# An embedding gather with position add: whole-sequence stores in place of half-sequence stores

## The chip, the cores and the metric

The kernel runs on one core of a Trainium2 chip. The metric is device time in microseconds (us) of a run. Five runs of the kernel before gave 177.66, 179.09, 178.35, 179.17 and 179.04 us: a median of 179.04.

## What is computed

32 sequences of 512 token indices pick rows of 512 floats (2 KB) from a table of 50,000 rows; the row of the token's position is added:

```
token_embed = embedding_table[indices]        # (32, 512, 512) f32
return (token_embed + position_embed)         # position_embed (512, 512)
```

There is no matrix product. 32 x 512 x 2 KB = 33.55 MB are read from the table and as many are written; all else is small.

## The kernel before, in words

**Tiling.** A sequence b is a tile ("slot") of 128 partitions by K = 4 rows by 512 floats: partition p holds tokens 4p to 4p+3, so that the 8 KB of a partition are contiguous in the output, and the 1 MB of a sequence too. There are 23 slots (SLOTS); sequence b uses slot b % 23, so only sequences 23 to 31 use a slot again, and those of 0 to 8.

**Order.** The unit of work is a pair (b, k): the 128 tokens of row k in every partition, 256 KB. The list `order` (lines 64 to 66) fixes the sequence of the 128 units, numbered g: first k = 0, 1 of sequences 0 to 3 (FIRST = 4), then k = 2, 3 of these, then k = 0 to 3 of each of the sequences 4 to 31. Everything is written out by hand; no scheduler moves it.

**POOL** (lines 118 to 138) issues one indirect DMA for each unit: it gathers 128 rows of 2 KB into the slot. Ten semaphores ("lanes") take turns, and gather g waits until gather g-10 has landed (line 138). Gather 0 waits for the first indices, gather 16 for the turned indices (line 123), and the first gather of sequence 23, g = 92, until all stores of sequences 0 to 8 have landed (line 126).

**DVE** (lines 141 to 155) copies the position rows once from SBUF to PSUM, turns the indices of all sequences with one transpose, and adds the position rows to each unit in place as soon as its gather has landed. Each add increments `s_add`.

**ACT** (lines 158 to 165) issues the stores, all on its own queue, from the list `stores` (lines 67 to 72): each entry says after how many adds, which sequence, at which row k, and how many rows. The queue is worked through in order, and each store waits for its count of `s_add` (line 165). In the kernel before a store is half a sequence: two rows k of each partition, 4 KB from each partition, 512 KB in all. The first halves of sequences 0 and 1, and all of sequence 31, are stored by single rows (256 KB). That makes 60 stores of 512 KB and 8 of 256 KB.

**Loads.** SP's queue loads the first sequence's indices, ACT's queue the position rows (two loads of 512 KB) and the other indices. At the end POOL clears semaphores after the last add, and ACT waits for the last stores (lines 169 to 175).

Of the kernel before, what the change touches and what calls it, by code (L numbers as in the profile page):

```python
# [1 line left out]

# [4 lines left out]

P = 128
K = 4
SLOTS = 23  # L10
LANES = 10
FIRST = 4
Q = 32


@with_exitstack
def kernel(
    ctx: ExitStack,
    tc: tile.TileContext,
    indices: bass.AP,  # L20
    embedding_table: bass.AP,
    position_embed: bass.AP,
    out: bass.AP,
):

    nc = tc.nc
    f32 = mybir.dt.float32
    i32 = mybir.dt.int32
    add = mybir.AluOpType.add

    B, S = indices.shape
    V, D = embedding_table.shape
    assert S == P * K and B == 32
    J = P // Q  # L40
    assert B == Q, "indices are turned in squares of 32"


    idx_words = indices.bitcast(i32)
    idx_first = idx_words[0:FIRST].rearrange("b (p w) -> p b w", p=P)
    idx_rows = idx_words.rearrange("b (j w) -> b j w", j=J)
    out_rows = out.rearrange("b (p k) d -> b p k d", k=K)
    pos_rows = position_embed.rearrange("(p k) d -> p k d", k=K)
    table = embedding_table[:, :]

    def sbuf(name, shape, dtype):
        return nc.alloc_sbuf_tensor(name, shape, dtype).ap()

    idx0 = sbuf("idx0", [P, FIRST, 2 * K], i32)
    idx_raw = sbuf("idx_raw", [P, 2 * Q * K], i32)
    idx_t = sbuf("idx_t", [P, K, B], i32)
    pos_sb = sbuf("pos_sb", [P, K, D], f32)
    slots = [sbuf(f"slot{n}", [P, K, D], f32) for n in range(SLOTS)]
    pos_ps = nc.alloc_psum_tensor("pos_ps", [P, K, D], f32).ap()

    half = K // 2
    order = [(b, k) for h in range(2) for b in range(FIRST)
             for k in range(h * half, (h + 1) * half)]
    order += [(b, k) for b in range(FIRST, B) for k in range(K)]
    stores = []
    for g, (b, k) in enumerate(order):
        if (b <= 1 and k < half) or b == B - 1:
            stores.append((g + 1, b, k, 1))  # L70
        elif k % half == half - 1:
            stores.append((g + 1, b, k + 1 - half, half))

    sems = []

    def sem(name):
        sems.append(nc.alloc_semaphore(name))
        return sems[-1]

    s_first, s_next, s_raw = sem("s_first"), sem("s_next"), sem("s_raw")  # L80
    s_pos = [sem(f"s_pos{h}") for h in range(2)]
    s_gather = [sem(f"s_gather{n}") for n in range(LANES)]

    reused = range(B - SLOTS)
    s_out, s_idx, s_ps = sem("s_out"), sem("s_idx"), sem("s_ps")
    s_add, s_rest, s_pool = sem("s_add"), sem("s_rest"), sem("s_pool")
    nums = [x.num for x in sems]
    assert nums == list(range(nums[0], nums[0] + len(nums)))
    early, late = range(nums[0], nums[-3]), range(nums[-3], nums[-1] + 1)

    def rounds(g):
        return 16 * (g // LANES + 1)

    def load(out, in_, done, engine=nc.scalar):
        return engine.dma_start(out=out, in_=in_).then_inc(done, 16)

    def load_pos(h):
        part = slice(h * half, (h + 1) * half)
        return load(pos_sb[:, part, :], pos_rows[:, part, :], s_pos[h])

    for ins in (
        load(idx0[:, 0, :], idx_first[:, 0, :], s_first, engine=nc.sync),
        load_pos(0),
    ):
        tc.no_tile_sem_insts.add(ins.ins.name)
    tc.close()
    tc.compile()


    load(idx0[:, 1:, :], idx_first[:, 1:, :], s_next)
    for j in range(J):
        load(idx_raw[j * B : (j + 1) * B, :], idx_rows[:, j, :], s_raw)
    load_pos(1)


    nc.gpsimd.wait_ge(s_first, 16)
    for g, (b, k) in enumerate(order):
        if g == half:  # L120
            nc.gpsimd.wait_ge(s_next, 16)
        if g == FIRST * K:
            nc.gpsimd.wait_ge(s_idx, 1)  # L123
        if b == SLOTS and k == 0:
            done = sum(1 for x in stores if x[1] in reused)
            nc.gpsimd.wait_ge(s_out, 16 * done)
        if b < FIRST:
            where = idx0[:, b, 2 * k : 2 * k + 1]
        else:
            where = idx_t[:, k, b : b + 1]  # L130
        ins = nc.gpsimd.indirect_dma_start(  # L131
            out=slots[b % SLOTS][:, k, :],
            out_offset=None,
            in_=table,
            in_offset=bass.IndirectOffsetOnAxis(ap=where, axis=0),
        ).then_inc(s_gather[g % LANES], 16)
        if g >= LANES:
            ins._wait_ge(s_gather[g % LANES], rounds(g - LANES))


    for g, (b, k) in enumerate(order):
        if g == 7:
            nc.vector.transpose(  # L143
                out=idx_t[:],
                in_=idx_raw[:].rearrange("r (q k w) -> r k q w", k=K, w=2)[:, :, :, 0],
            )._wait_ge(s_raw, 16 * J).then_inc(s_idx, 1)
        if b == 0:
            nc.vector.tensor_copy(out=pos_ps[:, k, :], in_=pos_sb[:, k, :])._wait_ge(  # L148
                s_pos[k // half], 16
            ).then_inc(s_ps, 1)  # L150
            nc.vector.wait_ge(s_ps, k + 1)
        part = slots[b % SLOTS][:, k, :]
        nc.vector.tensor_tensor(  # L153
            out=part, in0=part, in1=pos_ps[:, k, :], op=add
        )._wait_ge(s_gather[g % LANES], rounds(g)).then_inc(s_add, 1)


    rest = 0
    for adds, b, at, n in stores:
        done = s_out if b in reused else s_rest  # L160
        rest += b not in reused
        nc.scalar.dma_start(
            out=out_rows[b][:, at : at + n, :],
            in_=slots[b % SLOTS][:, at : at + n, :],
        )._wait_ge(s_add, adds).then_inc(done, 16)

    nc.gpsimd.wait_ge(s_add, len(order))
    nc.gpsimd.drain()  # L170
    nc.gpsimd.dma_reset(early)
    nc.gpsimd.sem_clear(early).then_inc(s_pool, 1)
    nc.scalar.wait_ge(s_pool, 1)
    nc.scalar.wait_ge(s_rest, 16 * rest)
    nc.scalar.sem_clear(late)

# [1 line left out]
_INS = ['indices', 'embedding_table', 'position_embed']  # L178
_OUTS = [((32, 512, 512), 'float32')]


# [23 lines left out]
```

## Time and profile before

| | |
|---|---|
| median of five runs | 179.04 us (177.66 to 179.17) |
| the profiled execution, its time | 179.19 us |
| its span in the profile | 173.9 us |
| POOL busy | 121.4 us, 70% of the span, 132 instructions |
| DVE busy | 90.6 us, 52%, 133 instructions |
| DMA | 68.34 MB in 21,059 packets, mean 393 GB/s |
| chain that ended last | POOL 68%, issue 23%, DMA 6%, DVE 1% |
| stores | 60 of 512 KB and 8 of 256 KB, on ACT's queue |

The span is what the profiler records of the program; the time of the execution is 5.3 us longer. The chain that ended last is followed back from the last instruction; "issue" in it is time in which an engine waited for nothing that the profile shows. In the rows by line, "xN" is the count, then come busy time and mean ns of one, then idle time before them and what ended it. In the rows by slice, each digit is a fortieth of the span, in tenths of busy time. The DMA engines are 16, shared by all queues; queue 0 is that of POOL's gathers, queue 10 that of ACT's DMAs, queue 1 SP's. In the stretches, a DMA share of over 1 comes from packets of one engine that overlap a little in the records.

### The profile page before, as it was taken

To read this page: it belongs to the slowest core of one execution; us is meant where nothing else is said; L and a number is where in the kernel's file an instruction comes from. 1 tells how busy PE (TensorE), PEld (TensorE's weight loads), DVE (VectorE), ACT (ScalarE), POOL (GpSimd) and SP (SyncE) were. 2 spreads that over 40 slices of the span, in tenths; PEclk is the share of its full clock that TensorE was granted. 3 is DMA by queue.
4 is the path that set the end of the run, shared out by engine and by line. 5 is a ranking of instruction groups with operands and counts; after the bars stand their busy time and mean duration, and the time that the engine had idled before them with its cause. 6 is when DMAs were issued, how large, how long until landed. Compare 5 with 4: busy or idle time off the path is not lost.

```text
span 173.9 us, 387 instructions
## 1 busy us (share of the span) xinstructions
DVE 90.6 (52%) x133; POOL 121.4 (70%) x132
## 2 busy tenths in 40 slices
DVE  0343945544645555564556555555555465546451
POOL 2777777777777777777777777777777777777400
DMA  4889999999999999999999999999999999999997
GB/s 137 277 268 366 302 360 408 400 397 417 418 414 411 421 418 418 418 417 420 420 419 418 417 419 420 415 418 418 413 419 415 419 418 419 414 417 419 417 420 272
DMA packets 21059, 68.34 MB, mean 393 GB/s; under 512 B 3776, under 2 KB 3904, under 8 KB 21056
## 3 DMA queue, kind: packets, MB, share of 16 engines
q0 software_dynamic: 10240, 33.56, 49.8%
q10 hardware_dynamic: 10672, 34.75, 49.4%
q1 hardware_dynamic: 144, 0.00, 0.0%
q14 instruction: 3, 0.02, 0.0%
HBM read 34.75 MB, written 33.55 MB: 393 GB/s over the span
## 4 chain that ended last, share of the span: by engine, by line
POOL 68%; issue 23%; DMA 6%; DVE 1%; POOLq 0%
POOL slot L131 68%; DMA slot<-in_embedding_table_dram,idx_t 5%; DMA idx<-in_indices_dram 1%; DVE slot L153 1%; POOLq L123 0%
## 5 line engine op out<-in xcount | busy, mean ns | idle before, releaser
L131 POOL DMA_INDIRECT slot<-in_embedding_table_dram,idx_t x112 | 105.9, 946 | 34.1 <-issue 34.1
L153 DVE TENSOR_TENSOR slot<-slot,pos_ps 128x512 f32<-128x512 f32 x128 | 87.8, 688 | 76.1 <-issue 55.3
L131 POOL DMA_INDIRECT slot<-in_embedding_table_dram,idx x16 | 15.3, 954 | 7.4 <-issue 4.6
L148 DVE COPY pos_ps<-pos_sb 128x512 f32<-128x512 f32 x4 | 2.8, 690 | 4.2 <-DMA pos_sb<-in_position_embed_dram 4.2
L143 DVE STREAM_TRANSPOSE idx_t<-idx_raw 128x128 int32<-128x128 int32 x1 | 0.4, 400 | 0.0
L189 POOL MEMSET const-float32-0.0<- 128x1 f32 x1 | 0.1, 98 | 0.2 <-issue 0.2
L189 POOL MEMSET const-uint8-127<- 128x1 uint8 x1 | 0.1, 118 | 0.0
L189 POOL MEMSET const-bfloat16-1.0<- 128x1 bf16 x1 | 0.1, 113 | 0.0
L189 POOL MEMSET const-float32-1.0<- 128x1 f32 x1 | 0.1, 104 | 0.0
## 6 DMA issues: line engine op xcount, KB each, us to landing
out_dram<-slot ACTq DMA_DIRECT2D x60, 512.0 KB
out_dram<-slot ACTq DMA_DIRECT2D x8, 256.0 KB
slot<-in_embedding_table_dram,idx_t POOLq DMA_INDIRECT x112
pos_sb<-in_position_embed_dram ACTq DMA_DIRECT2D x2, 512.0 KB, 3.4
slot<-in_embedding_table_dram,idx POOLq DMA_INDIRECT x16
idx_raw<-in_indices_dram ACTq DMA_DIRECT2D x4, 32.0 KB
idx<-in_indices_dram SPq DMA_DIRECT2D x1, 4.0 KB, 2.3
idx<-in_indices_dram ACTq DMA_DIRECT2D x1, 12.0 KB
```

What stands on the lines that cost most here:

```text
L131: ins = nc.gpsimd.indirect_dma_start(out=slots[b % SLOTS][:, k, :], out_offset=None, in_=table, in_offset=bass.IndirectOffsetOnAxis(ap=whe ...
L143: nc.vector.transpose(out=idx_t[:], in_=idx_raw[:].rearrange("r (q k w) -> r k q w", k=K, w=2)[:, :, :, 0],)._wait_ge(s_raw, 16 * J).then_ ...
L148: nc.vector.tensor_copy(out=pos_ps[:, k, :], in_=pos_sb[:, k, :])._wait_ge(s_pos[k // half], 16).then_inc(s_ps, 1)
L153: nc.vector.tensor_tensor(out=part, in0=part, in1=pos_ps[:, k, :], op=add)._wait_ge(s_gather[g % LANES], rounds(g)).then_inc(s_add, 1)
L189: nc = _bacc.Bacc("TRN2", target_bir_lowering=False, num_devices=1)
```

## The change

Sequences 5 to 27 are stored whole: one DMA of 1 MB after the fourth add, in place of two of 512 KB after the second and the fourth. A limit on the length of the last dimension (half x D x 4 = 4096) is given to all stores, so that the 8 KB of a partition go as two descriptors of 4 KB; the halves and single rows are not longer than that. Sequences 0 to 4 and 28 to 31 keep their stores, and gathers, adds, lanes and slots stay as they were. The number of stores that gather 92 waits for is counted from the list, so it follows.

```diff
     for g, (b, k) in enumerate(order):
         if (b <= 1 and k < half) or b == B - 1:
             stores.append((g + 1, b, k, 1))
+        elif FIRST < b < B - 4:
+            if k == K - 1:
+                stores.append((g + 1, b, 0, K))
         elif k % half == half - 1:
             stores.append((g + 1, b, k + 1 - half, half))
...
         nc.scalar.dma_start(
             out=out_rows[b][:, at : at + n, :],
             in_=slots[b % SLOTS][:, at : at + n, :],
+            max_dma_last_dim=half * D * 4,
         )._wait_ge(s_add, adds).then_inc(done, 16)
```

In the order of the instructions only ACT's queue differs: after the four single rows come 8 halves, 23 whole sequences (128 x 2 x 1024 floats), 6 halves and four single rows, 45 stores in all.

## The prediction

> **What bounds the kernel now.** I read the page from the top, then the waits, then the timeline at both ends, then the busy time by stretches. The page of the kernel before:
>
> ```profile
> POOL 2777777777777777777777777777777777777400
> DMA  4889999999999999999999999999999999999997
> ...
> q0 software_dynamic: 10240, 33.56, 49.8%
> q10 hardware_dynamic: 10672, 34.75, 49.4%
> ...
> L131 POOL DMA_INDIRECT slot<-in_embedding_table_dram,idx_t x112 | 105.9, 946 | 34.1 <-issue 34.1
> L153 DVE TENSOR_TENSOR slot<-slot,pos_ps 128x512 f32<-128x512 f32 x128 | 87.8, 688 | 76.1 <-issue 55.3
> ```
>
> Two things are full. POOL never looks full (7 tenths), but the 946 ns of each gather are followed by 34.1 / 112 = 0.30 us for which no wait is named, so a gather costs it 1.25 us and 128 of them 160 us. The DMA engines are full as well: queue 0 (the gathers) and queue 10 (the stores, and the first loads) fill 49.8% and 49.4% of all 16 engines. DVE needs 0.69 us of each 1.25 us and has slack. In the view of the waits POOL's line is
>
> ```profile
> POOL slot L131 <- issue: 38.7, 127, 0.3
> ```
>
> The longest idle time before any gather after the first is 0.3 us: no gather has ever waited for its lane (line 138) or for a slot (line 126). The timeline gives the delay between a gather's issue and its add, for the first gather and for the last:
>
> ```profile
> 3.30 1.08 POOL L131 DMA_INDIRECT slot<-in_embedding_table_dram,idx  x1 [2.86 <-DMA idx<-in_indices_dram]
> ...
> 7.51 0.69 DVE L153 TENSOR_TENSOR slot<-slot,pos_ps 128x512 f32<-128x512 f32 x1 [2.65 <-DMA slot<-in_embedding_table_dram,idx]
> ```
>
> ```profile
> 162.22 0.94 POOL L131 DMA_INDIRECT slot<-in_embedding_table_dram,idx_t  x1 [0.30 <-issue]
> ...
> 170.17 0.69 DVE L153 TENSOR_TENSOR slot<-slot,pos_ps 128x512 f32<-128x512 f32 x1 [0.45 <-issue]
> ```
>
> It is 4.2 us for the first and 7.95 us for the last; gather 44 (issued at 58.43, added at 66.50) already had 8.07. So about 3.8 us of other transfers lie ahead of each gather, and this stock neither grows nor shrinks from about 60 us on. Busy time by stretches (columns: length, DVE, POOL, clock, DMA share, GB/s) says why:
>
> ```profile
> 10.00:15.00 5.00, 1.50 (x4) 3.78 (x5) 1.00 0.87 295
> 15.00:20.00 5.00, 3.77 (x7) 3.78 (x5) 1.00 0.99 353
> 20.00:25.00 5.00, 3.04 (x5) 3.78 (x5) 1.00 0.98 320
> ...
> 40.00:45.00 5.00, 2.97 (x5) 3.78 (x5) 1.00 1.03 417
> ...
> 100.00:120.00 20.00, 11.08 (x17) 15.13 (x17) 1.00 1.03 418
> 140.00:160.00 20.00, 11.04 (x17) 15.12 (x17) 1.00 1.03 418
> ```
>
> POOL asks for 262,144 B per 1.25 us, 209.7 GB/s, and the stores for as much again: 419.4. The DMA delivers 417 to 418. The end is therefore POOL's last gather (162.2 + 0.94 = 163.2) plus the time to drain what is queued: 173.9 - 163.2 = 10.7 us. Only two things move the end: POOL's cadence, or how much is left to drain, which is DMA time wasted or saved before.
>
> **The change, step by step.** I sum against the profiled execution: 179.19 us, a span of 173.9 and 5.3 us around it. The median of the five runs, 179.04, is 0.15 us lower; I carry the same difference over.
>
> *Fewer instructions on ACT.* Sequences 5 to 27 take 23 store instructions for 46, 68 become 45. Each issue takes 338 ns on ACT's queue, which does nothing else at that time and stands waiting for an add. 0, from 0 on both sides.
>
> *Fewer semaphore packets.* The data stay the same: 4 KB pieces, 23 x 256 of them, since the new limit (half x D x 4 = 4096 B) cuts the 8 KB row of a partition in two. What goes is one completion packet per engine for each dropped store: 23 per engine. The trace's packet records show 4 B packets at 9 ns and 4 KB packets at 159 ns (medians). 23 x 9 ns = 0.2 us saved. If starting and closing a transfer costs more than its record, the nearest row is the mean packet of queue 10, 0.494 x 16 x 173.9 us / 10,672 = 129 ns: 23 x 0.129 = 3.0 us saved. Nor can a loss come from removing packets. I take -0.2, by the row that has just this packet; ends 0 and -3.0.
>
> *The first half of each sequence waits for the second.* No wait is added in count, but the value waited for is two adds later, 2 x 1.25 = 2.5 us (37.64 to 40.37, so 2.73 us, for sequence 5). Behind the waiting store on ACT stand only later stores, which need later adds anyway. Who waits for a store? The slot wait at gather 92, issued at 118.45: it needs sequences 0 to 8, and the last of their gathers starts at 47.2, is added by about 56 and stored within a few us, so some 55 us of slack. And the end, where nothing is moved: sequences 28 to 31 keep their halves and quarters, and the 16 gathers of them span 20 us before POOL ends. What is left is the stock of work in the DMA: up to 512 KB, 256 KB on average, of store bytes is withheld. The stock that a gather finds ahead is 3.8 us, at 418 GB/s about 1.6 MB, so the mean leaves no dry engine; the first time, at 37.6 us, the stock is still being built (398 GB/s between 35 and 40 us, against the 419.4 that is asked for). Cover gone, the withheld 512 KB are 524,288 / 418,000 = 1.25 us of idle DMA, paid once, as POOL keeps its pace and the stock is larger from then on. I take the mean, 256 KB, 0.63 us; ends 0 and 1.25, and more in the first rival.
>
> *Stores come in bursts of 1 MB each 5 us.* A gather may find 8 more store packets per engine ahead of it: 8 x 159 ns = 1.27 us. Gather g waits on its lane for gather g-10, 12.5 us after that one's issue; with 7.95 + 1.27 = 9.2 us there are 3.3 us of slack. 0 for POOL, and the adds' shift ends with the halves of sequence 28. If the cover went, POOL would wait by what is above 12.5 us.
>
> The Trainium skill speaks for the change in "DMA: Bandwidth & Descriptors", Rules for kernel authors: it wants at least 1 MiB in a DMA and many small ones made one. By that page's fixed cost of about 2 us per DMA (Anatomy of one DMA), 23 fewer would be an estimated 46 us; the plateau of 418 GB/s with 512 KB stores contradicts it, because many DMAs are in flight together. The same page speaks against the change in Queues, rings and completion order: an engine drains a whole packet, typically 9 to 17 descriptors, of one queue before it turns to the other. By this rule a store's turn would grow from 9 to 17 descriptors, no view here shows it, and the sum would be as it is, since the burst term above already has a gather wait that long.
>
> **Sum:** -0.2 + 0.63 = +0.4 us on 179.19, 179.6; for the median of runs 179.04 + 0.4 = **179.4 us**. My forecast is no change that counts; 0.5% of 179, 0.9 us, is about what a measurement of this kernel can tell from none.
>
> **Rivals.** *Slower: the store queue runs dry in each period.* 1 MB at half of 418 GB/s takes 5.0 us, just the period, so every delay between a store's issue and its first byte opens a gap in which only gathers run. A 512 KB load takes 3.4 us from issue to landing, 1.25 us of it bytes, so the gap is at most 2.1 us. The rows of 10 to 25 us, where stores are sparse, give 295, 353 and 320 GB/s, mean 323, 23% less. At half the gap 1.05 x 0.23 x 23 = 5.6 us. The loss lengthens the gathers' delay and so refills the stock, which heals it; at the latest when the delay has grown by its 4.4 us of slack to the lanes' 12.5 us, and past that point POOL itself would wait. So +0.9 to +4.4, 181.4 in the middle. It decides if the gathers queued at the end of a store are worth less than the gap. For it: the three rows. Against: POOL fed those early stretches from a small stock, delays were 6.4 to 6.9 us and not 8.
>
> *Faster: closing a transfer costs an engine more than 9 ns.* Then up to 3.0 us go: 179.04 - 3.0 = 176.0 at best, 177.5 in the middle. For it: the engines are full, so whatever they don't do comes off the stock. Against: the DMA share is 1.03, the packets stand end to end with no room for hidden costs; and POOL's pace caps the gain at the stock, 7.95 - 4.2 = 3.8 us.
>
> *The limit does not cut.* Were rows moved in 8 KB pieces, queue 10 would have 23 x 128 = 2,944 packets fewer again and a store would get more of an engine per turn. The bytes are the same, so it is the forecast's time, within the ends above.
>
> **How the numbers follow.** Forecast, with the uncut case, 0.57: 178.2 to 179.9. Slower rival 0.26: 179.9 to 183.4. Faster rival 0.17: 176.0 to 178.1. The range leaves a tenth out on each side: 177.6, inside the faster rival, to 181.8, a little past the middle of the slower. Chances by 0.5%: faster 0.17, within 0.57, slower 0.26.
>
> **What would show it.** Right: queue 10 with 23 x 16 = 368 packets fewer, 10,304; POOL's idle still 0.3 us at most; the last gather starting at 162.2; 417 to 419 GB/s in the slices from 45 us; a last add near 170.5. The burst term: delays between 8 and 9.3 us in mid-run. The slower rival: slices at 400 GB/s or under after 40 us, delays of 10 us and more, or POOL idle before a gather for over 0.3 us with the DMA as releaser. The faster rival: delays that fall below 7.5 us towards the end while GB/s stay. I am wrong if POOL's cadence itself changes, because the stores lengthen its 946 ns.

## The result, and the profile after

The changed kernel takes 179.13 us (median of 52 runs) where the kernel before, run beside it, takes 179.03 (94 runs). The ratio is 1.0030, with an interval of 1.0020 to 1.0039: 0.54 us slower (0.36 to 0.70), where +0.4 was forecast. The ratio compares the runs as a whole: their means are 0.53 us apart, the medians only 0.10, because the times of both kernels lie in groups some 0.7 us apart (near 178.4, 179.1 and 179.75). The profiled execution took 179.21 us with a span of 174.4, half a microsecond more than before.

The page of the changed kernel, in the lines that answer to those of before (all lines of code have moved down by three):

```profile
POOL 2777777777777777777777777777777777777300
DMA  4889999999999999999999999999999999999997
GB/s 135 287 265 366 301 350 407 410 371 412 401 403 415 418 412 401 420 418 420 419 418 420 420 419 421 419 419 418 421 420 418 419 421 420 420 420 419 419 418 272
...
q0 software_dynamic: 10240, 33.56, 49.8%
q10 hardware_dynamic: 10304, 34.75, 49.1%
...
L134 POOL DMA_INDIRECT slot<-in_embedding_table_dram,idx_t x112 | 105.9, 946 | 34.1 <-issue 34.1
L156 DVE TENSOR_TENSOR slot<-slot,pos_ps 128x512 f32<-128x512 f32 x128 | 87.1, 687 | 77.1 <-issue 58.3
```

Queue 10 has the 10,304 packets that were forecast, 368 fewer, so the row of 8 KB was cut in two and only completion packets went. POOL's lines are unchanged, and so is its line in the view of the waits:

```profile
POOL slot L134 <- issue: 38.7, 127, 0.3
```

No gather waited for a lane or a slot. The difference stands at the end. Timeline, last gather and last add:

```profile
162.20 0.95 POOL L134 DMA_INDIRECT slot<-in_embedding_table_dram,idx_t  x1 [0.30 <-issue]
...
170.48 0.69 DVE L156 TENSOR_TENSOR slot<-slot,pos_ps 128x512 f32<-128x512 f32 x1 [0.71 <-issue]
```

POOL issued its last gather at the same time, 162.2, and the add came 0.31 us later than before. More was left to drain. Where it had been left behind is seen in the slices of the page above (371, 412, 401, 403 from the ninth slice on, 35 to 52 us). The kernel before has 397, 417, 418, 414 there:

```profile
GB/s 137 277 268 366 302 360 408 400 397 417 418 414 411 421 418 418 418 417 420 420 419 418 417 419 420 415 418 418 413 419 415 419 418 419 414 417 419 417 420 272
```

It is seen in the busy time by stretches too (length, DVE, POOL, clock, DMA share, GB/s). First the kernel before, in stretches not shown yet:

```profile
35.00:45.00 10.00, 5.35 (x8) 7.56 (x9) 1.00 1.03 408
45.00:60.00 15.00, 7.71 (x12) 11.35 (x13) 1.00 1.03 415
60.00:80.00 20.00, 11.01 (x16) 15.12 (x17) 1.00 1.03 419
...
120.00:140.00 20.00, 10.93 (x16) 15.12 (x17) 1.00 1.03 417
```

Then the changed kernel:

```profile
35.00:45.00 10.00, 5.36 (x10) 7.56 (x9) 1.00 1.01 396
45.00:60.00 15.00, 7.64 (x12) 11.34 (x13) 1.00 1.02 408
60.00:80.00 20.00, 11.23 (x17) 15.13 (x17) 1.00 1.03 413
80.00:100.00 20.00, 10.83 (x17) 15.13 (x17) 1.00 1.03 419
...
120.00:140.00 20.00, 10.91 (x17) 15.12 (x17) 1.00 1.03 420
```

The difference lies between 35 and 80 us: 12 x 10 + 7 x 15 + 6 x 20 = 345 GB/s x us, 345 KB (here thousands of bytes) that the DMA engines didn't move. From 80 us on it moves a little more than before. The same can be counted from the trace's packet records, as the bytes landed up to a time, less those of the kernel before at that time (the gathers laid over each other):

| KB behind the kernel before at | 40 us | 50 | 60 | 80 | 100 | 120 | 160 |
|---|---|---|---|---|---|---|---|
| changed kernel | 128 | 204 | 236 | 344 | 336 | 316 | 220 |

Not all of this is the work of the change. The kernel before issued the first half of sequence 5, which the changed kernel holds back, at 37.67 us, and its bytes are missed from 41 us on: in all six kernels of this document that hold it back, queue 10 is 264 or 268 KB behind at 42 us, and 92 KB or less at 41. So the 128 KB at 40 us, with a dip to 295 and 303 GB/s between 37.5 and 38.5 us (377 and 369 before), come too early to be due to the change. The ten other runs stand between some 145 KB ahead and 85 KB behind at 40 us: a single profile carries an offset of some 100 KB from its start. From 40 us on the changed kernel falls another 216 KB behind and makes up 124 of them by 160 us. The 220 KB that stay would be 220 x 1024 / 418,000 = 0.54 us, but 128 of them are offset, and without them it is 0.23 us; that the count meets the 0.54 us of the runs is chance. The time rests on 146 runs. The count shows where bytes are lost when they are well over 100 KB, as with the larger doses below.

### The profile page after: what moved, and what is told of

Its sections match the earlier page's. It is cut to its first block, busy times and chain, and to the rows that moved or that the text cites. A ratio compares the mean times of both kernels' runs of the same rounds, so it can differ in the third digit from the quotient of the medians.

```text
span 174.4 us, 364 instructions
## 1 busy us (share of the span) xinstructions
DVE 89.9 (52%) x133; POOL 121.4 (70%) x132
## 3 DMA queue, kind: packets, MB, share of 16 engines
q10 hardware_dynamic: 10304, 34.75, 49.1%
## 4 chain that ended last, share of the span: by engine, by line
POOL 64%; issue 25%; DMA 6%; DVE 4%
POOL slot L134 64%; DMA slot<-in_embedding_table_dram,idx_t 4%; DVE slot L156 4%; DMA idx<-in_indices_dram 1%
```

## Experiments

**Theory.** In mid-run the DMA engines have no spare rate: POOL asks for 419.4 GB/s and they move 418. A store that is held back takes its bytes out of the queued work. While the store queue then stands empty, the gathers alone must keep the engines full, and POOL feeds them only half of the rate. The engines run short until POOL, which keeps its pace, has queued as much more as is held back. By this theory that time is paid once, while the stock grows, and never given back. **Rivals:** a price at each release (a gap each period), a price of the 1 MB transfer itself, and the number of transfers.

All ratios are against the kernel before on the same chip, whose time differs by chip (175.1 to 179.0 us) though its span doesn't (173.8 us on average on each).

### The release alone, and the transfer alone

`late_halves`: two halves, both after the fourth add.

```diff
+        elif FIRST < b < B - 4:
+            if k == K - 1:
+                stores += [(g + 1, b, 0, half), (g + 1, b, half, half)]
```

> The stores of sequences 5 to 27 are still two halves each, but both are issued after the fourth add; the number of transfers is that of the kernel before. Theory 1, withheld work (256 KB more held back on average, made up once while the stock of queued work builds): 0.63 us slower than before, about 0.2 us slower than the changed kernel. Theory 2, the form of the 1 MB transfer (17 entries of one queue in a row) is what costs: as before, within 0.2 us. Mid-run delay of the gathers by theory 1 near the 7.4 us of the changed kernel, by theory 2 near 8.0.

Measured: 1.0042 (1.0023 to 1.0060), 0.75 us slower. Bytes behind: 396 KB from 70 us on, 316 at 160. The time of release is all that differs from the kernel before, so the release makes the loss, without any 1 MB transfer. The delay that was to tell the theories apart can't do it. The gathers' mean delay from issue to add between gathers 60 and 112 is 7.1 us here, 7.4 in the changed kernel and 8.0 before, but it is 7.4 in `split_even` below, which holds nothing back. Between gathers 40 and 60 it is 7.3 in `pairs_late` and 8.2 in `whole_late`, whose stores up to there are those of the kernel before.

`whole_8k`: the changed kernel without the limit of 4096 B, so that a partition's row is one piece of 8 KB.

> Whole stores as in the changed kernel, without the limit, so that the 8 KB of a partition are one piece. If only the time of release counts: as the changed kernel, 0.3 to 0.6 us slower than before. If the length of a piece counts, gathers are held up longer behind each store packet (8 KB for 4 KB): later adds and over 1 us slower than before; or 8 packets fewer for each engine and store and a gain of a few tenths of a us on the changed kernel.

Measured: 1.0027 (1.0002 to 1.0051), 0.5 us slower, not to be told from the changed kernel. Queue 10 has 7,360 packets now. It falls further behind (560 KB at 100 us) and makes up more (348 left at 160 us); its stretch from 120 to 140 us has 422 GB/s. If the length of the piece moves single terms, they cancel within the interval.

### The dose

`pairs`: whole stores, released by pairs of sequences. `fours`: the same with 4 in place of 2.

```diff
+        elif 5 <= b < 28:
+            if k == K - 1 and ((b - 5) % 2 == 1 or b == 27):
+                first = b - (b - 5) % 2
+                stores += [(g + 1, x, 0, K) for x in range(first, b + 1)]
...
+            max_dma_last_dim=half * D * 4,
```

> Whole stores as in the changed kernel, but held back until the second sequence of a pair has been added (5 and 6, 7 and 8, ..., 25 and 26, then 27): 896 KB withheld on average, for 128 KB with halves. Theory 1, withheld work paid once: 768 KB more / 418 GB/s = 1.9 us less 0.2 us of packets = 1.7 us slower than before. Rival, a gap at each release that costs the same each time: 12 releases for 23, so half of the 0.5 + 0.2 us of the changed kernel less 0.2 us, 0.2 us slower. The loss by theory 1 shows as slices under 419 GB/s between 35 and 100 us, and not after.

> Stores released by groups of four sequences from 5 to 27 (the last group has three). Theory 1, the peak of what is held back grows by 4,096 - 512 = 3,584 KB, made up once: 8.8 us slower than before. By the mean that is held back (1,920 - 128 = 1,792 KB): 4.4 us. By a price for each release: 6 releases for 12, 1.6 us.

Measured: `pairs` 1.018 (1.0151 to 1.021), 3.2 us slower; `fours` 1.0415 (1.0372 to 1.0458), 7.3 us slower. The first is nearly twice what I expected by the mean that is held back, and close to the peak, 1,536 KB or 3.8 us; the second lies nearer to the peak's 8.8 us than to the mean's 4.4. The price for each release is out: it foretold 0.2 and 1.6 us. Another rival would be the bursts, two or four stores of 1 MB in a row that hold up the gathers. It is out for the main part of the loss: `fours` is 1,340 KB behind at 50 us, and its first release is issued at 51.6. Stretches of `pairs`:

```profile
35.00:45.00 10.00, 6.81 (x12) 7.56 (x9) 1.00 0.97 365
45.00:60.00 15.00, 7.72 (x13) 11.34 (x13) 1.00 0.99 373
60.00:80.00 20.00, 9.05 (x15) 15.12 (x17) 1.00 1.01 389
80.00:100.00 20.00, 10.71 (x17) 15.12 (x17) 1.00 1.02 416
100.00:120.00 20.00, 10.98 (x17) 15.13 (x16) 1.00 1.03 419
```

The same releases that cost 40 GB/s at 50 us cost nothing at 110 us. Note the DMA share of 0.97 to 1.01 in the poor stretches. In the first it is 6% below the 1.03 of the good ones, where the rate is 11% below the 408 of the kernel before. The 4 KB packets of the gathers take 179 ns there on average in the records, for 159 in the good stretches (the median is 159 in both), which would fit packets that wait and count as busy; no run shows that by itself. Here the GB/s must be read, not the share.

### The place, and whether it is given back

`whole_late` and `pairs_late` begin at sequence 16; `pairs_early` holds back 5 to 10 only. The cut is against `pairs`; `whole_late` releases each sequence by itself.

```diff
-        elif 5 <= b < 28:
+        elif 16 <= b < 28:        # pairs_late; pairs_early: 5 <= b < 11
```

> Whole stores as in the changed kernel, but only for sequences 16 to 27; 0 to 15 keep halves, so that the holding back begins at about 90 us, when the stock of queued work is complete. Theory 1 (what is held back at the peak has to be made up by queued work, paid once wherever it begins): 0.3 to 0.6 us slower than before, as the changed kernel, with the slow slices after 90 us. Rival, the mid-run stock covers it and only the build up to 70 us can lose: as before, within 0.2 us. Rival, a price for each release: 12 of 23, 0.25 us slower.

> Stores released by pairs of sequences, but only for sequences 16 to 27. Theory 1, the peak of what is held back grows by 1,536 KB, made up once: 1,536 KB / 418 GB/s = 3.7 us slower than before, as for pairs from sequence 5 on (3.2 us measured), with the bytes moved falling behind by 1.4 to 1.6 MB after 90 us. Rival, mid-run stock covers: under 1.5 us. Rival, a price for each release: 6 of 12, 1.6 us slower.

> Stores released by pairs of sequences only for 5 to 10 (three pairs), halves from 11 on. Theory 1, paid once and never given back, since the DMA has no spare rate afterwards: in the kernel with pairs throughout, the bytes moved had fallen 1,160 KB behind by 65 us, so 2.8 us slower than before. Rival, a price for each release: 3 of 12, 0.8 us slower. Rival, given back when the halves return: under 0.5 us.

Measured: `whole_late` 1.0029 (1.0006 to 1.0051), 0.5 us; `pairs_late` 1.0211 (1.0173 to 1.0249), 3.7 us; `pairs_early` 1.0169 (1.0131 to 1.0207), 3.0 us. All three fall where the theory put them, and the two with pairs leave no rival of those foretold. The interval of `whole_late`, 0.1 to 0.9 us, holds the price for each release (0.25) as well, so its time alone decides nothing. Its stretches show a loss that comes in one place, after 90 us, with the stock of mid-run complete:

```profile
90.00:100.00 10.00, 6.51 (x10) 7.56 (x9) 1.00 1.03 417
100.00:110.00 10.00, 4.98 (x8) 7.56 (x9) 1.00 1.02 390
110.00:120.00 10.00, 5.47 (x8) 7.56 (x9) 1.00 1.03 421
```

Microsecond by microsecond:

```profile
100.00:101.00 1.00, 0.86 (x2) 0.70 (x2) 1.00 1.06 434
101.00:102.00 1.00, 0.00 (x0) 0.89 (x1) 1.00 1.09 291
102.00:103.00 1.00, 0.38 (x1) 0.80 (x1) 1.00 0.97 283
103.00:104.00 1.00, 0.31 (x1) 0.69 (x2) 1.00 0.95 377
```

By the bytes the whole loss is this one dip of three microseconds, 303 KB against 418 GB/s. A whole store had been issued at 99.58 us, but from 101 to 103 us its queue moves 68 KB, for some 410 in an even share, and the gathers alone don't fill the engines. Eleven other releases of this kernel pass without such a dip; why this one didn't, no run here settles.

Three releases cost `pairs_early` nearly all that twelve cost `pairs`. After it has gone back to halves, the stretches show full rate, and the last gather and add show what that full rate can't mend:

```profile
162.23 0.95 POOL L135 DMA_INDIRECT slot<-in_embedding_table_dram,idx_t  x1 [0.30 <-issue]
...
172.65 0.69 DVE L157 TENSOR_TENSOR slot<-slot,pos_ps 128x512 f32<-128x512 f32 x1 [0.59 <-DMA slot<-in_embedding_table_dram,idx_t]
```

POOL is on time, and the delay is 10.4 us in place of 7.95; it was 9.1 at gather 60 and has grown rather than shrunk since. The stock is large enough for pairs, and stays, because the 419 to 420 GB/s that are moved from 80 us on are no more than POOL and the stores ask for. Bytes behind the kernel before (offsets of some 100 KB included):

| KB behind at | 50 us | 60 | 80 | 100 | 120 | 160 | held back more at the peak |
|---|---|---|---|---|---|---|---|
| changed kernel | 204 | 236 | 344 | 336 | 316 | 220 | 512 |
| whole_late | 56 | 48 | 36 | 52 | 328 | 220 | 512 |
| pairs | 436 | 936 | 1516 | 1572 | 1548 | 1452 | 1,536 |
| pairs_early | 676 | 1016 | 1284 | 1288 | 1272 | 1192 | 1,536 |
| pairs_late | -32 | -32 | 24 | 244 | 960 | 1364 | 1,536 |
| fours | 1340 | 2292 | 2704 | 2932 | 3124 | 3240 | 3,584 |

For the pairs and the fours, what is lost is about the growth of the peak: 0.8 to 1.0 of it, by the bytes at 160 us and by the time. For single sequences it is less, 0.4 to 0.6 of 1.25 us by the time, and by the bytes the offset is too large to say. Why the small dose pays a smaller share is not settled. Nor is it all paid at the first release: `pairs_late` still moves only 408 and 406 GB/s in the stretches from 120 to 160 us. The kernel with fours is limited most sharply around its first release, between 45 and 55 us, when it falls 1.9 MB behind in 10 us.

### The number of transfers, and the other direction

`split64`: halves at the times of before, each as two transfers of 64 partitions. `split_even`: the same, by every second partition. The counts that the waits look for follow in both.

```diff
+        parts = 2 if FIRST < b < B - 4 else 1
+        for h in range(parts):
+            rows = slice(h * P // parts, (h + 1) * P // parts)   # split64
+            rows = slice(h, P, parts)                            # split_even
...
+                out=out_rows[b][rows, at : at + n, :],
+                in_=slots[b % SLOTS][rows, at : at + n, :],
```

> Halves at the times of before, but each half of sequences 5 to 27 goes as two transfers of 64 partitions: 46 more transfers, 4 KB pieces as before, nothing withheld. Semaphore packets at 9 ns: 46 x 9 ns = 0.4 us slower than before. If opening and closing a transfer costs an engine the mean packet of 129 ns: 5.9 us slower. If the number of transfers costs nothing: no change.

> As split64, 46 more transfers at the times of before, but each of the two takes every second partition (0, 2, 4, ... and 1, 3, 5, ...) in place of the lower and the upper 64. If the number of transfers is what made split64 3.8% slower: the same, 6 to 7 us slower than before. If it was that one transfer read only half of the range of partitions: 46 x 9 ns = 0.4 us slower than before, up to 1 us.

Measured: `split64` 1.038 (1.0335 to 1.0424), 6.8 us slower; `split_even` 1.0022 (1.0004 to 1.0040), 0.39 us slower. By itself the first looked like a price of 148 ns for each transfer, above the upper end that I had given. The second has as many transfers, packets and semaphores, and costs 0.39 us / 46 = 8 ns each (1.5 to 15 by the interval), close to the 9 ns of the completion packet in the records. So the number was not the cause; taking the lower and the upper 64 partitions apart was. In the records of `split64` the 4 KB packets between 80 and 116 us take 163 ns on average (gathers) and 164 (stores), for 159 in the kernel before; single ones take up to 1,096 and 845 ns, for 488 and 162, though elsewhere in mid-run the kernel before has a gather packet of 1,355 too. The span of `split64` grew by 3.7 us on average, that of `split_even` by 0.4. The other 3 us of the time of `split64` lie around the span (8.5 us on average, for 5.1 in the kernel before on that chip), and what they are no run here settles. `split_even` ran on another chip, where only 1.5 us lie around the span of either kernel, so the 3 us may belong to the chip; the 3.7 us of span are what the two runs compare safely.

`single_rows`: sequences 5 to 27 stored by single rows, 256 KB after each add, in 2 KB pieces.

```diff
-        if (b <= 1 and k < half) or b == B - 1:
+        if (b <= 1 and k < half) or b == B - 1 or FIRST < b < B - 4:
             stores.append((g + 1, b, k, 1))
```

> Sequences 5 to 27 are stored by single rows, 256 KB after each add: 256 KB less held back at the peak than before, in 2 KB pieces. Theory 1 takes off up to 256 KB / 418 GB/s = 0.6 us; the packet records price the rest: 2 x (8 x 84 + 9) ns for two single rows, 8 x 159 + 9 ns for one half, 81 ns more for each of 46 halves, 3.7 us. Sum: 3.1 us slower than before. If the release time outweighed the packets it would be faster than before; if 46 more transfers cost as in split64, over 6 us slower.

Measured: 1.0114 (1.0084 to 1.0144), 2.0 us slower. The gathers' delay falls to 6.0 us, the smallest of all kernels, and nothing is behind at 60 us (10 KB), which agrees with less held back. Then it loses steadily, in stretches of before's 418:

```profile
80.00:100.00 20.00, 10.75 (x17) 15.13 (x17) 1.00 1.04 412
100.00:120.00 20.00, 11.26 (x17) 15.12 (x17) 1.00 1.04 412
120.00:140.00 20.00, 11.06 (x17) 15.13 (x17) 1.00 1.04 412
```

That is 1.4% less for 2 KB pieces. The packet records had priced 3.1% (81 ns in a period of 2.6 us on each engine), so the records of the short packets overstate them here; a part of this may be that they overlap more, with a share of 1.04 for 1.03. Halves lie between two losses, and no release that these runs point to beats the kernel before.

## Why the prediction was right, step by step

*What bounds it:* right. POOL's cadence stayed, its last gather started at 162.2 in every kernel run (up to 162.6), and every loss showed as work left to drain.

*ACT's issues, 0:* nothing in the runs speaks against it; ACT's time was not varied by itself.

*Fewer semaphore packets, -0.2 us:* right in size. 46 more cost 0.39 us (0.07 to 0.70) in `split_even`; the upper end of 129 ns, and with it the faster rival, is out. (The fixed cost of about 2 us that the prediction takes from the Trainium skill, "DMA: Bandwidth & Descriptors", Anatomy of one DMA, is fitted there on DMAs issued by POOL, not on stores like these, and 46 of it would be 92 us.) That the changed kernel is 0.2 us faster than `late_halves`, which differs from it by the 23 transfers, agrees, but the two intervals overlap.

*The first half waits, +0.63 us:* the term that decided, and right in mechanism: the release time makes the loss, and not each release, while POOL keeps its pace. Its size was partly luck. I took the mean of what is held back. The dose shows that the peak counts: by the mean, `pairs` should have lost 1.9 us and lost 3.2. For whole sequences the measured 0.54 + 0.2 = 0.74 us lies between the mean's 0.63 and the peak's 1.25, so the mean came close where a sum with the peak would have said +1.05. The reason that I gave for cover was wrong: 1.6 MB of queued work did not cover 512 KB, as `whole_late` shows with a complete stock. Nor is the work that is issued and not yet landed a good measure of cover. By the packet records about 1.9 MB of it stood there during the dip of `whole_late`, half of it a store of which hardly a byte had moved, while the changed kernel comes down to 1.2 MB in mid-run (1.5 before) and moves over 360 GB/s then.

*Bursts, gathers delayed to 8 to 9.3 us:* not seen. The mean delay of the profiled execution is 7.4 us, below the 8.0 of the kernel before, but executions with the same stores differ by as much (7.3 and 8.2, as above), so no sign is shown. I had looked at the gathers behind a burst and not at those ahead of it: while a sequence is held back the store queue runs empty (in the records it moves 12 and 8 KB in the two half microseconds from 41.0 us, for 100 in an even share) and the gathers have the engines to themselves. The longer turn of one queue, by the rule weighed in the prediction, did not show in the time: `late_halves` and the changed kernel agree within their intervals. The term was set to 0 in the sum, so the sum did not suffer.

*The slower rival:* right about gaps in the store queue and about the healing, wrong in making them a price per period: `pairs` has half the releases and six times the loss, `pairs_early` three releases and over five times. (The middle of its +0.9 to +4.4 us is 181.7, not 181.4; nothing else rests on it.)

## What to carry to other kernels

Where an engine feeds a saturated DMA at a fixed pace, holding back an output is paid by the growth of the peak that is held back, over the DMA rate, and not by the number of releases. Here it cost 0.8 to 1.0 of that for 1.5 MB and more and about half for 512 KB, wherever in the run it began, and little of it came back. Count bytes landed against the kernel before over time: it tells a loss that is paid once from one paid each period, which the totals don't. Look first at how far two executions of the same code lie apart in such a count; here it is some 100 KB, or 0.25 us. Before a cost is put down to the number of transfers, keep the number and change their shape.

## What was not expected of the hardware

- 46 stores of 512 KB cut into the lower and the upper 64 partitions cost 6.8 us, of which 3.7 us lie inside the span; cut into even and odd partitions, 0.39 us.
- The DMA share falls less than the rate: 0.97 at 365 GB/s and 0.99 at 373 in `pairs`, for 1.03 at 408 to 420. A share near 1 does not show that the engines are kept full.
- From 80 us on, stores in 8 KB pieces moved 418 to 422 GB/s by stretches, in 4 KB pieces (kernels before and after) 417 to 420, in 2 KB pieces 412 to 413.
